# First mixer of a two-layer trunk: one softmax division moved into the head's norm, and rotations and value splits done on pairs of tiles

## The chip, the cores and the metric

The kernel runs on one core of one Trainium2 chip. The metric is the device time of one execution in microseconds (us). The core's engines each follow their own instruction list in order and wait for one another by semaphores: TensorE (PE in the profile, with its weight loads as PEld), VectorE (DVE), ScalarE (ACT), GpSimd (POOL) and SyncE (SP), which here issues most of the DMAs.

## The reference, cut to what matters

The reference is a trunk of two layers on a sequence of 256 rows of width 1024, with a context of 256 rows. Only the first layer's mixer is touched: differential attention with 8 heads (128 value columns each, two maps of 64 columns), joined with a gated unit and followed by a product with `w_out`. All of it is float32.

```python
q_x, k_x, v_x, gu_x, gv_x = split(hx @ w_in)          # rows of x
k_c, v_c = split(hc @ w_in[:, ...])                    # rows of the context
q_x, k_x = apply_rope(q_x), apply_rope(k_x)            # rotate halves of 64 columns
k_all, v_all = concat([k_c, k_x]), concat([v_c, v_x])  # 512 rows
# per block of 128 query rows and head, m = 0, 1:
p = softmax(q[m] @ k[m].T * scale)                     # 128 x 512, two maps
a = p[0] - lam * p[1]
o = a @ v                                              # 128 x 128
# head_rms:
o = o * rsqrt(mean(o * o) + 1e-5) * g * (1 - lam_init)
```

After the mixer come a norm, a PEER block (top-k routing over 16384 experts), and the second layer with a pooling mixer and another PEER block. None of that changes.

## The kernel before, in words

All weight matrices stream in as "items": tiles of 128x1024 float32. For each item SyncE loads a `raw` tile (four buffers, line 54), ScalarE copies it to a rounded `hi` (line 61) and VectorE subtracts to get `lo` (line 63); there are three `hi`/`lo` pairs (`RING`). A product is then three matmul passes, hi by hi, hi by lo and lo by hi. `run_items` writes the order by hand: for each item it first emits the splits of up to two items ahead (`ahead`), then the item's matmuls (`run`), then work that was put off by the item before (`settle` runs what `defer` collected), then the item's `after`. The engines' lists follow this order of emission, so what stands behind a waiting instruction on its engine waits too.

The first mixer works in four groups g of two heads. A group is six items:

- two k items (t = 0, 1). `transposed` (line 598) makes 24 matmuls of 256 columns for the rows of x into `p[:, :256]` and 24 for the context into `p[:, 256:]`; p is one of three PSUM buffers of one bank (`pa`). In `after`, `rope` rotates the x half, and `parts` splits the context half with one ScalarE copy (line 154) and one VectorE subtraction (line 155).
- two q items: 24 matmuls each into half a bank, then `rope`.
- two v items, of which the second does all the work: four blocks b of 24 matmuls (line 837), each into a bank of its own and each with its own `parts`.

`rope` (lines 678 to 691) swaps groups of 32 partitions with four ScalarE copies from PSUM into `sw` (line 683), multiplies p by a table row on VectorE (line 685), and defers four more VectorE steps, `rest`: a multiplication (688), an addition (689), and the split into hi and lo (193, 194). Its two scratch tiles have three buffers each. Both engines read the same bank here, and the framework puts accesses of two engines to one bank one behind the other.

The attention itself is cut into 20 "units" (`unit`, called by `units`), one at a time beside the items: in group g at four places (k item 0, k item 1, blocks 0 and 2 of v), and for units 13 to 19 in the first items of the product with `w_out`. Unit u makes the scores of (head, query block) number u, transposes those of u - 2 (`turn`), multiplies by v for a finished head (`mix`), and at u = 7, 11, 15, 19 takes the norm of a group (`rms`). `scores` (lines 694 to 715) does six matmuls into two banks and then, for each map m: VectorE's negated maximum (707), ScalarE's exponential with the row sum in a column (709), VectorE's reciprocal of that sum (710). Then VectorE scales the second reciprocal by -lam (712), the second map by it (713), and adds the first map times its reciprocal (714).

Beside this VectorE adds up three vectors from `ada_w` (`ada_step`: one step loads a 128x1024 tile `aw` into one of three buffers, line 366, and does one multiply-add over the tile loaded before it, line 375; two steps after each k item, one after others). At the end of a vector TensorE takes column sums (line 382). After the last unit's norm the memory of the attention is closed, and only then SyncE loads the residual rows and `grow` (line 876) for the norm that follows the mixer (line 219).

Of the kernel before, what the change touches and what calls it, by code (L numbers as in the profile page):

```python
# [11 lines left out]
FT = mybir.dt.float32  # L12
# [22 lines left out]
class Build:  # L35
# [425 lines left out]
    def first(self):  # L461
# [216 lines left out]
        def rope(dst, h, p, x):  # L678
            T = st["K"]

            sw = T.tile([128, 256], FT, name="rp", bufs=3)
            for r in range(0, 128, 32):
                nc.scalar.activation(sw[r:r + 32], p[r ^ 32:(r ^ 32) + 32], AF.Copy)
            t = T.tile([128, 256], FT, name="rt1", bufs=3)
            nc.vector.tensor_mul(t, p, st["rope"][:, x, 0])

            def rest():
                nc.vector.tensor_mul(sw, sw, st["rope"][:, x, 1])
                nc.vector.tensor_add(t, t, sw)
                self.split_v(dst[0][:, h, :256], dst[1][:, h, :256], t)  # L690
            self.defer(rest)


        def scores(g, h, nb):
            T = st["T"]
            s = slice(128 * nb, 128 * nb + 128)
            mx = T.tile([128, 2, 4], FT, name="amx", bufs=3)
            e = []
# [7 lines left out]
            for m, p in enumerate(ps):  # L706
                nc.vector.tensor_reduce(mx[:, m, 0:1], p, axis=AX.X, op=OP.max, negate=True)
                x = T.tile([128, 512], FT, name="ex", bufs=6)
                nc.scalar.activation(x, p, AF.Exp, bias=mx[:, m, 0:1], accum_out=mx[:, m, 2:3])
                nc.vector.reciprocal(mx[:, m, 3:4], mx[:, m, 2:3])  # L710
                e.append(x)
            nc.vector.tensor_mul(mx[:, 1, 3:4], mx[:, 1, 3:4], st["nlam"])
            nc.vector.tensor_scalar(e[1], e[1], mx[:, 1, 3:4], None, op0=OP.mult)
            nc.vector.scalar_tensor_tensor(e[0], e[0], mx[:, 0, 3:4], e[1], op0=OP.mult, op1=OP.add)
# [28 lines left out]
        def rms(g):  # L743
# [3 lines left out]
            for h in range(2):  # L747
                for nb in range(2):
                    nc.tensor.matmul(p[:, 2 * h + nb:2 * h + nb + 1], sq[:, h, 128 * nb:128 * nb + 128], self.ones,
                                     start=True, stop=True)  # L750
            ms = T.tile([128, 4], FT, name="ms", bufs=2)
            nc.vector.tensor_scalar(ms, p[:, :4], 1.0 / 128, EPS, op0=OP.mult, op1=OP.add)
# [31 lines left out]
        for g in range(4):  # L784
            for t in range(2):
                def run(hi, lo, t=t, g=g):
                    p = self.pa()
                    transposed(hi, lo, [(p[:, :256], self.h)])
                    if g and t == 0:
                        self.settle()  # L790
                        units()
                    transposed(hi, lo, [(p[:, 256:], hc)])
                    st["p"] = p

                def after(g=g, t=t):
                    if t == 0:
                        T = st["K"]
                        st["k", g] = [T.tile([128, 2, 512], FR, name=f"kT{i}", bufs=2) for i in range(2)]
                        st["q", g] = [T.tile([128, 2, 256], FR, name=f"qT{i}", bufs=2) for i in range(2)]
                    ada_step(2)  # L800
                    k = st["k", g]
                    rope(k, t, st["p"][:, :256], 0)
                    self.parts(k[0][:, t, 256:], k[1][:, t, 256:], st["p"][:, 256:])
# [10 lines left out]
            for t in range(2):  # L814
                def run(hi, lo):
                    st["p"] = self.pa()
                    transposed(hi, lo, [(st["p"][:, :256], self.h)])

                def after(g=g, t=t):
                    ada_step()  # L820
                    rope(st["q", g], t, st["p"][:, :256], 1)
                self.item(w[n], run, after=after)
                n += 1
            for t in range(2):
                def run(hi, lo, t=t, g=g):
# [5 lines left out]
                    for b in range(4):  # L831
                        p = self.pa()[:, :256]
# [6 lines left out]
                        self.parts(v[0][:, b], v[1][:, b], p)  # L839
# [612 lines left out]
```

## Time and profile before

| | |
|---|---|
| time, median of 3 runs | 2065.9 us (2065.89 to 2066.82) |
| the profiled execution | 2066.66 us, span 2064.7 us |
| mean granted TensorE clock | 0.978 of full speed |
| PE busy | 1977.2 us (96%) |
| DVE busy | 1572.4 us (76%) |
| ACT busy | 978.5 us (47%) |
| POOL busy | 379.1 us (18%) |
| DMA | 389.93 MB, 189 GB/s over the span |

The span runs from the first to the last instruction of the profiled execution. A busy share is an average over stages with different limits. Times inside a stage are given from the start of the span; the groups of the first mixer lie between some 65 and 252 us, its product with `w_out` from there to some 308 us. Ends of matmuls are modelled, so that neighbouring matmuls overlap on paper. In a timeline row the first two numbers are start and duration, and a bracket tells how long the engine had been idle before it and what released it. In a row of waits the three numbers are the total, the count and the longest.

### The profile page before, as it was taken

The numbers are of one execution on the slowest core, as the hardware profiler recorded it, in microseconds if no ns is written. First come the engines' busy times: TensorE is split into PE (matmuls) and PEld (weight loads), VectorE is DVE, ScalarE is ACT, GpSimd is POOL, SyncE is SP. The second block draws the span as 40 slices with busy tenths as digits, with TensorE's granted clock in tenths as the row PEclk, the third lists the DMA queues.
The fourth block names the chain that finished last, engine by engine and source line by source line (L and its number), as shares of the span: only waits on it lengthen the run. The fifth ranks groups of instructions, "written<-read, shape, count | busy, mean of one in ns | idle before, by whom it ended". The sixth has DMA issues, their size and how long they took to land.

```text
span 2064.7 us, 34190 instructions
## 1 busy us (share of the span) xinstructions
PE 1977.2 (96%) x13348; PEld 1781.8 (86%) x13348; DVE 1572.4 (76%) x2820; ACT 978.5 (47%) x1398; POOL 379.1 (18%) x171
## 2 busy tenths in 40 slices
PE   8899888999999999999999889999999999999997
PEld 4888767999999998888878679999999998888886
DVE  6878867999888857777776767999888755555566
ACT  6444435454544444444445454454544444444443
POOL 0100006785000000000011427892000000000031
PEclk9999998999999999999999989999999999999999
DMA  8533244455444457888876445555444555665663
GB/s 305 209 134 133 82 143 164 154 176 172 156 156 149 154 190 258 289 293 305 285 275 214 175 142 174 168 180 164 154 154 147 172 183 193 193 195 193 212 232 128
DMA packets 108177, 389.93 MB, mean 189 GB/s; under 512 B 12776, under 2 KB 12904, under 8 KB 108016
## 3 DMA queue, kind: packets, MB, share of 16 engines
q1 hardware_dynamic: 105992, 384.37, 55.3%
q10 hardware_dynamic: 2024, 3.38, 0.5%
q8 instruction: 104, 1.70, 0.3%
q14 instruction: 57, 0.47, 0.1%
HBM read 384.55 MB, written 3.16 MB: 188 GB/s over the span
## 4 chain that ended last, share of the span: by engine, by line
PE 63%; DVE 26%; issue 6%; ACT 3%; DMA 1%; POOL 1%; SPq 0%; ACTq 0%; DVEq 0%; POOLq 0%
PE pa L311 25%; PE px L311 8%; PE pa L941 8%; PE pa L945 7%; PE pa L942 7%; DVE lo L63 2%; PE pt L1093 2%; ACT hi L61 1%; DVE oh L1020 1%; DVE oh L1025 1%; DVE topi L971 1%; DVE sc L972 1%; DVE topi L974 1%; PE pa L837 1%; DVE idx L1026 1%
## 5 line engine op out<-in xcount | busy, mean ns | idle before, releaser
L61 ACT ACTIVATE hi<-raw 128x1024 fp32r<-128x1024 f32 x599 | 633.0, 1059 | 573.7 <-PE px L311 359.6
L63 DVE TENSOR_TENSOR lo<-raw,hi 128x1024 fp32r<-128x1024 f32 x487 | 614.1, 1263 | 363.6 <-ACT hi L61 362.3
L941 PE MATMUL pa<-h,hi 128*128 128x256 f32 x2304 | 578.1, 289 | 2.1 <-DVE h L280 2.1
L942 PE MATMUL pa<-h,hi 128*128 128x256 f32 x2304 | 566.4, 284 | 0.5 <-DVE h L281 0.5
L311 PE MATMUL pa<-hi,h 128*128 128x512 f32 x1524 | 472.1, 391 | 1.3 <-ACT h L278 1.2
L941 PEld LDWEIGHTS pa<-h,hi 128*128 128x128 f32 x2304 | 442.0, 192 | 2.9 <-DVE h L280 2.9
L942 PEld LDWEIGHTS pa<-h,hi 128*128 128x128 f32 x2304 | 442.9, 192 | 1.0 <-issue 1.0
L311 PEld LDWEIGHTS pa<-hi,h 128*128 128x128 f32 x1524 | 286.3, 188 | 64.1 <-issue 1.7
L945 PE MATMUL pa<-h,lo 128*128 128x256 f32 x2304 | 323.6, 283 | 0.0
L63 POOL TENSOR_TENSOR lo<-raw,hi 128x1024 fp32r<-128x1024 f32 x112 | 287.8, 2587 | 79.2 <-ACT hi L61 78.8
L945 PEld LDWEIGHTS pa<-h,lo 128*128 128x128 f32 x2304 | 298.1, 192 | 0.0
L311 PE MATMUL pa<-lo,h 128*128 128x512 f32 x762 | 255.7, 390 | 0.0
L1227 POOL TENSOR_SCALAR ln_g<-ln_g 128x1024 f32<-128x1024 f32 x2 | 5.6, 2776 | 1144.0 <-DMA ln_g<-in_ln_g 1144.0
L311 PE MATMUL px<-hi,h 128*128 128x512 f32 x508 | 197.7, 389 | 0.0
L311 PEld LDWEIGHTS pa<-lo,h 128*128 128x128 f32 x762 | 143.4, 188 | 30.0
L1107 ACT ACTIVATE A<-pt 128x256 f32<-128x256 f32 (+31 forms) x182 | 50.9, 310 | 226.6 <-DVE A L1105 217.4
L311 PEld LDWEIGHTS px<-hi,h 128*128 128x128 f32 x508 | 95.3, 188 | 19.7
L1084 DVE TENSOR_TENSOR m<-e,gd 128x512 f16<-128x512 f16 x256 | 105.2, 452 | 2.2
L311 PE MATMUL px<-lo,h 128*128 128x512 f32 x254 | 98.8, 389 | 0.0
L375 DVE SCALAR_TENSOR_TENSOR aacc<-aw,csil,aacc 128x1024 f32<-128x1024 f32 x70 | 89.4, 1278 | 0.1
L1093 PE MATMUL pt<-m,e 128*128 128x128 f16 x1024 | 81.6, 220 | 3.1 <-DVE m L1084 0.7
L155 DVE TENSOR_TENSOR h<-A,h 128x1024 fp32r<-128x1024 f32 (+1 forms) x66 | 81.0, 1227 | 1.4 <-ACT h L154 1.4
(369 smaller groups left out, 2178.5 us busy)
## 6 DMA issues: line engine op xcount, KB each, us to landing
raw<-in_uT SPq DMA_DIRECT2D x256, 512.0 KB, 3.5
raw<-in_peer_v SPq DMA_DIRECT2D x256, 512.0 KB, 4.3
aw<-in_ada_w SPq DMA_DIRECT2D x80, 512.0 KB, 5.4
raw<-in_w_in SPq DMA_DIRECT2D x32, 512.0 KB, 4.7
raw<-in_wq SPq DMA_DIRECT2D x32, 512.0 KB, 3.7
raw<-in_ab_w_out SPq DMA_DIRECT2D x12, 512.0 KB, 3.5
raw<-in_ada_w SPq DMA_DIRECT2D x8, 512.0 KB, 5.7
xraw<-in_ada_w SPq DMA_DIRECT2D x8, 512.0 KB, 4.9
```

What stands on the lines that cost most here:

```text
L61: nc.scalar.activation(hi, it["raw"], AF.Copy)
L63: eng.tensor_sub(lo, it["raw"], hi.bitcast(FT))
L155: self.nc.vector.tensor_sub(lo, src, hi.bitcast(FT))
L311: nc.tensor.matmul(acc[2 * nb + a // 512], s[x], w[:, a:b], start=i == 0 and part == 0, stop=i == last and part == 2)
L375: nc.vector.scalar_tensor_tensor(st["acc"], w, c, st["acc"], op0=OP.mult, op1=OP.add)
L837: nc.tensor.matmul(p, h(k, s)[x], tiles[k // 4][y][:, 256 * (k % 4):256 * (k % 4) + 256], start=part == 0 and k == 0, stop=part == 2 and k ...
L941: mm(out, hi[:, cs], hh, start=k == 0, stop=False)
L942: mm(out, hi[:, cs], hl, start=False, stop=False)
L945: mm(out, lo[:, cs], self.h(k)[0], start=False, stop=k == 7)
L1084: nc.vector.tensor_tensor(v4(x), v4(st["e1"][:, s]), wide(st["gd"][i], ch, 4), op=OP.mult)
L1093: nc.tensor.matmul(p[:, 128 * j:128 * j + 128], e2[:, j], m[i][:, j], start=i == 0, stop=i == 1)
L1107: nc.scalar.activation(x[:, e:], y[:, e:], AF.Copy, scale=1.0 / 4096)
```

## The change

- `scores`: the first map is no longer divided by its sum. Its sums go to a tile of four columns per group (`asum`). The second map is scaled by (first sum / second sum) times -lam and added to the undivided first map, so a head's output is too large by the first sum. One reciprocal and one pass over 128x512 fall away; the other small step takes two column operands.
- `rms`: the head's norm divides that factor out. For this the small constant in the norm is multiplied by the squared sum: two VectorE steps on 128x4 where there was one.
- k items: the x halves of both items go into one bank and the context halves into another; `rope` and `parts` then run once for the pair, in the second item's `after`, on 512 columns. q items: both into one bank, `rope` once for the pair. The scratch tiles of `rope` have one buffer of twice the size.
- v blocks: two blocks share a bank, and `parts` runs once for two.

The matmuls, the splits of weight tiles and all DMAs stay as they are.

```diff
-        def rope(dst, h, p, x):
+        def rope(dst, p, x):
+
             T = st["K"]
-            sw = T.tile([128, 256], FT, name="rp", bufs=3)
+            sw = T.tile([128, 2, 256], FT, name="rp", bufs=1)
             for r in range(0, 128, 32):
                 nc.scalar.activation(sw[r:r + 32], p[r ^ 32:(r ^ 32) + 32], AF.Copy)
-            t = T.tile([128, 256], FT, name="rt1", bufs=3)
-            nc.vector.tensor_mul(t, p, st["rope"][:, x, 0])
+            t = T.tile([128, 2, 256], FT, name="rt1", bufs=1)
+
+            def row(i):
+                return st["rope"][:, x, i][:, None].to_broadcast([128, 2, 256])
+            nc.vector.tensor_mul(t, p, row(0))
             def rest():
-                nc.vector.tensor_mul(sw, sw, st["rope"][:, x, 1])
+                nc.vector.tensor_mul(sw, sw, row(1))
                 nc.vector.tensor_add(t, t, sw)
-                self.split_v(dst[0][:, h, :256], dst[1][:, h, :256], t)
+                self.split_v(dst[0][:, :, :256], dst[1][:, :, :256], t)
...
+            if h == nb == 0:
+                st["sum", g] = T.tile([128, 4], FT, name="asum", bufs=3)
+            sums = st["sum", g][:, 2 * h + nb:2 * h + nb + 1], mx[:, 1, 2:3]
...
-                nc.scalar.activation(x, p, AF.Exp, bias=mx[:, m, 0:1], accum_out=mx[:, m, 2:3])
-                nc.vector.reciprocal(mx[:, m, 3:4], mx[:, m, 2:3])
+                nc.scalar.activation(x, p, AF.Exp, bias=mx[:, m, 0:1], accum_out=sums[m])
                 e.append(x)
-            nc.vector.tensor_mul(mx[:, 1, 3:4], mx[:, 1, 3:4], st["nlam"])
-            nc.vector.tensor_scalar(e[1], e[1], mx[:, 1, 3:4], None, op0=OP.mult)
-            nc.vector.scalar_tensor_tensor(e[0], e[0], mx[:, 0, 3:4], e[1], op0=OP.mult, op1=OP.add)
+            nc.vector.reciprocal(mx[:, 1, 3:4], sums[1])
+            nc.vector.tensor_scalar(mx[:, 1, 3:4], mx[:, 1, 3:4], st["nlam"], sums[0], op0=OP.mult, op1=OP.mult)
+            nc.vector.scalar_tensor_tensor(e[0], e[1], mx[:, 1, 3:4], e[0], op0=OP.mult, op1=OP.add)
...
+            sm = st.pop(("sum", g))
             ms = T.tile([128, 4], FT, name="ms", bufs=2)
-            nc.vector.tensor_scalar(ms, p[:, :4], 1.0 / 128, EPS, op0=OP.mult, op1=OP.add)
+            nc.vector.scalar_tensor_tensor(sm, sm, EPS, sm, op0=OP.mult, op1=OP.mult)
+            nc.vector.scalar_tensor_tensor(ms, p[:, :4], 1.0 / 128, sm, op0=OP.mult, op1=OP.add)
...
                 def run(hi, lo, t=t, g=g):
-                    p = self.pa()
-                    transposed(hi, lo, [(p[:, :256], self.h)])
+                    if t == 0:
+                        st["pk"] = [self.pa() for _ in range(2)]
+                    cs = slice(256 * t, 256 * t + 256)
+                    transposed(hi, lo, [(st["pk"][0][:, cs], self.h)])
...
-                    transposed(hi, lo, [(p[:, 256:], hc)])
-                    st["p"] = p
+                    transposed(hi, lo, [(st["pk"][1][:, cs], hc)])
                 def after(g=g, t=t):
-                    if t == 0:
+                    ada_step(2)
+                    if t:
...
-                    ada_step(2)
-                    k = st["k", g]
-                    rope(k, t, st["p"][:, :256], 0)
-                    self.parts(k[0][:, t, 256:], k[1][:, t, 256:], st["p"][:, 256:])
+                        p = [x.rearrange("p (a b) -> p a b", a=2) for x in st["pk"]]
+                        rope(k, p[0], 0)
+                        self.parts(k[0][:, :, 256:], k[1][:, :, 256:], p[1])
...
                     ada_step()
-                    rope(st["q", g], t, st["p"][:, :256], 1)
+                    if t:
+                        rope(st["q", g], st["p"].rearrange("p (a b) -> p a b", a=2), 1)
...
-                        p = self.pa()[:, :256]
+                        if b % 2 == 0:
+                            pv = self.pa()
+                        p = pv[:, 256 * (b % 2):256 * (b % 2) + 256]
...
-                        self.parts(v[0][:, b], v[1][:, b], p)
+                        if b % 2:
+                            self.parts(v[0][:, b - 1:b + 1], v[1][:, b - 1:b + 1], pv.rearrange("p (a b) -> p a b", a=2))
```

## Rows read from the trace of the kernel before

**Rows 1.** The page's chain of work that ended last, as shares of the whole span by engine.

```profile
PE 63%; DVE 26%; issue 6%; ACT 3%; DMA 1%; POOL 1%; SPq 0%; ACTq 0%; DVEq 0%; POOLq 0%
```

**Rows 2.** Busy time by stretch: the stretch, its length, then busy us and instructions of each engine, the granted clock, the DMA share and GB/s. The four stretches are those of the mixer from the v block of group 0 into the product with `w_out`.

```profile
93.00:131.00 38.00, 34.22 (x246) 30.37 (x246) 29.85 (x55) 14.17 (x31) 0.00 (x0) 0.96 0.47 159
131.00:177.00 46.00, 41.34 (x286) 38.17 (x287) 37.38 (x70) 21.79 (x50) 0.00 (x0) 0.85 0.44 149
177.00:230.00 53.00, 46.98 (x368) 43.47 (x366) 42.90 (x87) 23.90 (x53) 0.00 (x0) 0.97 0.32 110
230.00:278.00 48.00, 42.23 (x256) 35.50 (x257) 37.47 (x93) 22.86 (x49) 0.00 (x0) 0.89 0.24 77
```

**Rows 3.** Who waited for whom between 78 and 310 us: total us, times, longest.

```profile
DVE amx L710 <- ACT ex L709: 27.5, 32, 1.2
ACT kT L154 <- DVE rt L685: 17.6, 7, 4.2
...
PE pa L837 <- ACT hi L61: 11.9, 6, 3.7
...
PE pa L837 <- DVE lo L63: 4.7, 3, 3.2
...
DVE nlam L510 <- ACT sl L508: 1.1, 1, 1.1
...
DVE amx L707 <- PE pt L705: 0.4, 1, 0.4
```

**Rows 4.** VectorE's timeline over one unit of scores, from the first maximum to the first instruction behind the unit.

```profile
244.02 0.68 DVE L707 TENSOR_REDUCE amx<-pt 128x1 f32<-128x512 f32 x1
245.55 0.16 DVE L710 RECIPROCAL amx<-amx 128x1 f32<-128x1 f32 x1 [0.84 <-ACT ex L709]
245.63 0.67 DVE L707 TENSOR_REDUCE amx<-pt 128x1 f32<-128x512 f32 x1
247.15 0.16 DVE L710 RECIPROCAL amx<-amx 128x1 f32<-128x1 f32 x1 [0.85 <-ACT ex L709]
...
248.06 0.75 DVE L714 SCALAR_TENSOR_TENSOR ex<-ex,amx 128x512 f32<-128x512 f32 x1
248.73 0.75 DVE L155 TENSOR_TENSOR v<-pa,v 128x256 fp32r<-128x256 f32 x2
```

**Rows 5.** ScalarE's timeline in the same unit.

```profile
246.34 0.69 ACT L709 ACTIVATE ex<-pt,amx 128x512 f32<-128x512 f32 x1 [0.82 <-DVE amx L707]
246.92 0.19 ACT L709 ACTIVATION_READ_ACCUMULATOR ex<-pt,amx 128x1 f32 x1
247.01 0.65 ACT L154 ACTIVATE v<-pa 128x256 fp32r<-128x256 f32 x2
```

**Rows 6.** Groups of instructions between 100 and 330 us by line and shape: busy us, mean ns of one | idle before.

```profile
L683 ACT ACTIVATE rp<-pa 32x256 f32<-32x256 f32 x48 | 18.0, 376 | 5.3 <-PE pt L705 4.6
L154 ACT ACTIVATE aT<-pt 128x512 fp32r<-128x512 f32 x16 | 9.6, 597 | 2.6 <-PE pt L724 2.5
...
L194 DVE TENSOR_TENSOR cat<-og,cat 128x512 fp32r<-128x512 f32 x4 | 2.8, 692 | 0.1
L759 DVE TENSOR_TENSOR og<-og,pt 128x512 f32<-128x512 f32 x4 | 2.7, 678 | 0.0
...
L194 DVE TENSOR_TENSOR kT<-rt,kT 128x256 fp32r<-128x256 f32 x6 | 2.6, 425 | 0.2
...
L193 DVE CAST kT<-rt 128x256 fp32r<-128x256 f32 x6 | 1.8, 294 | 0.2
...
L193 DVE CAST cat<-og 128x512 fp32r<-128x512 f32 x4 | 1.7, 426 | 0.1
...
L185 DVE TENSOR_SCALAR rs_t<-rs_t,rs_r 128x1 f32<-128x1 f32 x2 | 0.4, 212 | 0.1
```

**Rows 7.** VectorE's timeline around the first k item of group 3.

```profile
219.50 0.41 DVE L685 TENSOR_TENSOR rt<-pa,rope 128x256 f32<-128x256 f32 x1
220.36 0.42 DVE L155 TENSOR_TENSOR kT<-pa,kT 128x256 fp32r<-128x256 f32 x1 [0.45 <-ACT kT L154]
221.31 1.22 DVE L63 TENSOR_TENSOR lo<-raw,hi 128x1024 fp32r<-128x1024 f32 x1 [0.52 <-ACT hi L61]
222.45 0.42 DVE L688 TENSOR_TENSOR rp<-rp,rope 128x256 f32<-128x256 f32 x1
...
224.03 1.28 DVE L375 SCALAR_TENSOR_TENSOR aacc<-aw,csil,aacc 128x1024 f32<-128x1024 f32 x1
```

**Rows 8.** TensorE's timeline: where a product with v began late, and the end of a k item in group 2.

```profile
93.82 1.22 PE L837 MATMUL pa<-lo,h 128*128 128x256 f32 x4 [3.18 <-DVE lo L63]
...
163.36 1.12 PE L598 MATMUL pa<-hc,lo 128*128 128x256 f32 x8
...
231.34 1.22 PE L837 MATMUL pa<-hi,h 128*128 128x256 f32 x4 [3.72 <-ACT hi L61]
```

**Rows 9.** VectorE's timeline in groups 0 and 2: two steps of `ada` after the second k item of group 0, and the first multiplication of `rope` for the first k item of group 2.

```profile
78.12 2.60 DVE L375 SCALAR_TENSOR_TENSOR aacc<-aw,csil,aacc 128x1024 f32<-128x1024 f32 x2
...
167.36 0.42 DVE L685 TENSOR_TENSOR rt<-pa,rope 128x256 f32<-128x256 f32 x1
```

**Rows 10.** DMA issues by line between 60 and 290 us: count, KB each, median us from issue to landing.

```profile
aw<-in_ada_w SPq DMA_DIRECT2D x24, 512.0 KB, 5.1
```

**Rows 11.** SyncE's timeline: two loads for `ada` in group 0, with the time that their issue took.

```profile
73.40 1.79 SPq L366 DMA_DIRECT2D aw<-in_ada_w  x2
```

More of the change, by code (lines that the diff above doesn't have):

```diff
@@ L791, in run @@
                         units()
-                    transposed(hi, lo, [(p[:, 256:], hc)])
-                    st["p"] = p
+                    transposed(hi, lo, [(st["pk"][1][:, cs], hc)])
                 def after(g=g, t=t):
-                    if t == 0:
+                    ada_step(2)
+                    if t:
                         T = st["K"]
-                        st["k", g] = [T.tile([128, 2, 512], FR, name=f"kT{i}", bufs=2) for i in range(2)]
+                        k = st["k", g] = [T.tile([128, 2, 512], FR, name=f"kT{i}", bufs=2) for i in range(2)]
                         st["q", g] = [T.tile([128, 2, 256], FR, name=f"qT{i}", bufs=2) for i in range(2)]
-                    ada_step(2)
-                    k = st["k", g]
-                    rope(k, t, st["p"][:, :256], 0)
-                    self.parts(k[0][:, t, 256:], k[1][:, t, 256:], st["p"][:, 256:])
+                        p = [x.rearrange("p (a b) -> p a b", a=2) for x in st["pk"]]
+                        rope(k, p[0], 0)
+                        self.parts(k[0][:, :, 256:], k[1][:, :, 256:], p[1])
                     if g and t:
@@ L814, in first, with run @@
             for t in range(2):
-                def run(hi, lo):
-                    st["p"] = self.pa()
-                    transposed(hi, lo, [(st["p"][:, :256], self.h)])
+                def run(hi, lo, t=t):
+                    if t == 0:
+                        st["p"] = self.pa()
+                    transposed(hi, lo, [(st["p"][:, 256 * t:256 * t + 256], self.h)])
                 def after(g=g, t=t):
                     ada_step()
-                    rope(st["q", g], t, st["p"][:, :256], 1)
+                    if t:
+                        rope(st["q", g], st["p"].rearrange("p (a b) -> p a b", a=2), 1)
                 self.item(w[n], run, after=after)
```

## The prediction

> **What bounds the kernel now.** I read the chain of waits first. Over the whole span it lies 63% on TensorE and 26% on VectorE [rows 1], and the page's 96% for PE would say that work on VectorE is free. That is an average over stages, so next comes the table of stretches for the mixer alone. There TensorE is idle for 38 - 34.2 = 3.8, 4.7, 6.0 and 5.8 us of the four stretches, 20.3 us together, and its granted clock is below one in all four [rows 2]. The two levels are 2.4 and 1.2 GHz. A mean clock of 0.85 over 46 us is 6.9 us of full-speed time lost, and 1.5, 1.6 and 5.3 in the others: 15.3, some of it inside the idle time. TensorE could therefore be 20 to 35 us faster here if it were never kept waiting.
>
> Then the list of waits, to see who keeps it waiting. Its products with v waited 11.9 us for `hi` and 4.7 for `lo` [rows 3], and the gaps stand at the first v block of a group (3.2 and 3.7 us) [rows 8]. The reverse wait hardly exists: VectorE waited 0.4 us for score matmuls [rows 3]. What VectorE does wait for is ScalarE: 27.5 us in 32 waits before the reciprocals, 0.85 us each. In group 2 TensorE had finished both k items at 164.5 us [rows 8], while VectorE came to the rotation of the first one at 167.4 [rows 9]. So from about 102 to 283 us VectorE's list, with its waits for the exponentials in it, is the limit, and TensorE stands still when `lo` or a tile behind it comes late. Time taken out of that list should move the end until TensorE itself is the limit.
>
> **The change, part by part, on VectorE's list.**
>
> *Scores.* A unit takes 248.73 - 244.02 = 4.71 us [rows 4]. Now both maxima are issued one behind the other and nothing between them waits. The exponential starts 0.71 after its maximum (245.63 to 246.34), the next ScalarE instruction can start 0.67 later (246.34 to 247.01), and the reciprocal follows its exponential by 0.81 (246.34 to 247.15) [rows 4, 5]. So the one reciprocal comes at 0.71 + 0.67 + 0.81 = 2.19. Then 0.20 for it, 0.25 for the small step with two column operands (0.21 long [rows 6]), and 0.67 for the last pass up to the next instruction (248.06 to 248.73). That is 3.31, a gain of 1.40 per unit, 22.4 in 16. The bounds: if the second maximum still had to wait for the first exponential, because both write one small tile, the unit would take 0.71 + 0.81 + 0.71 + 0.81 + 1.12 = 4.16 and the gain be 8.8. With a small step of 0.16 it is 23. I take 22.4; no instruction shown here lets me see the first of these cases.
>
> *Rotations.* On 256 columns one takes about 1.92: 1.58 for the deferred part (222.45 to 224.03 [rows 7]) and 0.34 for the first multiplication. By durations two of them are 2 x (0.41 + 3 x 0.425 + 0.294) = 3.96; on 512 columns it is 0.678 + 3 x 0.692 + 0.426 = 3.18 [rows 6]. I take 0.7 per pair, since neighbours overlap by some 0.1, and 5.6 for eight pairs. That no row shows a table row read twice by one instruction bounds it between 0 (two runs at the old price) and 6.4. On ScalarE the four copies go from 4 x 0.376 to 4 x about 0.6 per pair (the 512-column copy is 0.597 [rows 6]), 2.4 for 3.0; ScalarE is not the limit, so I count nothing.
>
> *Context halves of k.* Today ScalarE's copy of the context half waits for VectorE's multiplication of the x half, 17.6 us in seven waits [rows 3], because the two halves share a bank. VectorE then waits 0.45 for that copy, and again 0.52 for the `hi` that stands behind the copy on ScalarE [rows 7]. In the changed kernel the halves lie in two banks, and the copy can run early. I count 8 x 0.45 = 3.6, 4 x 0.5 = 2.0, and 4 x 0.15 for one subtraction in place of two. The table load for the exponential in group 0 stands behind the same copy, so VectorE's 1.1 us wait for `nlam` [rows 3] goes too.
>
> *Split of v and the norm.* Two subtractions of about 0.68 replace four of 0.42 per group, less overlap 0.15: 0.6 in all. The norm's extra step on four columns costs 0.2 four times: +0.8. Bounds for both together are minus 1 and plus 1.
>
> Sum on VectorE: 22.4 + 5.6 + 3.6 + 2.0 + 0.6 + 1.1 + 0.6 - 0.8 = 35.1 us.
>
> *What moves.* The rotation of the first k item now waits for the second item's matmuls. That costs nothing while VectorE comes to it later anyway, as in group 2 above. The Trainium skill speaks against it: PSUM — Partial Sum Buffer, in its section "PSUM bank collisions raise a hardware error", asks that two engines not touch one bank at a time, so a bank that holds both tiles can't be emptied while TensorE fills its second half. By that rule alone each pair would put about one k item of TensorE work in front of VectorE, some 6 us four times; the rows in which VectorE is behind say about zero, and the sum takes zero.
>
> A real cost is the order: all deferred steps of the k pair (2.5 us for 1.58) now stand between the two `lo` tiles that the first v block needs. That is 0.95 later per group, 3.8 in all.
>
> *From VectorE's sum to the end.* In the four stretches lie 15 units (21.0), seven pairs (4.9), six of the 0.45 and three of the 0.5 waits (4.2), and 0.5 net of the small terms: 30.6. Against it stand the 3.8, about 2 where VectorE will now reach the column sums of `ada` before TensorE has made them, and about 3 for hand-overs where the two engines are level, my estimate from the single gaps of 0.5 to 1 us. That leaves 21.8, inside TensorE's room of 20 to 35. In group 0 the gain is small: the second `ada` step after the k pair needs a tile issued at about 73.4 [rows 11] that takes 5.1 us [rows 10], so it can't start before 78.5, and it starts at 79.4 today [rows 9]. I count 0.9, plus 1.2 for the waits behind it, less the 0.95 already charged: 1.2. Unit 15, behind the stretches, gives 1.4. Together 21.8 + 1.2 + 1.4 = 24.4. What follows the mixer is the same program and only starts earlier. The profiled execution took 2066.7, 0.8 above the median of 2065.9: 2066.7 - 24.4 = 2042.3, and I say 2042.
>
> **The rivals.**
>
> 1. TensorE or the `hi` tiles become the limit early, and half of the gain is lost. For it: the stretches have only 20.3 us of plain idle time, and the clock may stay low. Against: a low clock came with gaps. Price: the waits for `hi` and `lo` alone are 16.6; with 4 us of them left the gain is about 12.6: 2054.
> 2. The second maximum still waits for the first exponential. The gain falls by 22.4 - 8.8 = 13.6 to 10.8: 2056. Against: the two use different columns.
> 3. No change: VectorE's time is hidden after all, as the page's 96% for PE has it. Against: the waits of PE in the mixer. 2063 to 2069.
> 4. Slower. The swap's scratch tile now has one buffer. The copies of the q pair on ScalarE can't start before the addition for the k pair has read it, and VectorE's multiplication waits for all four copies. Between that addition and the multiplication stand a cast, a subtraction, two `ada` steps and a `lo`, about 0.46 + 0.61 + 2 x 1.2 + 1.13 = 4.6 us, against 2.4 of copies, so by these rows nothing waits, and in group 3, with no `ada` steps left, 2.2 against 2.4. It decides only if `rope` waits 35.1 / 8 = 4.4 us or more per pair. At most it is the copies at 4 x 0.75 = 3.0 and the deferred 2.5, 5.5 for each of eight pairs: 44 - 35 = 9 slower, 2076.
>
> That the pairs are not run as such (two runs of 256 inside an instruction) is the lower bound of the rotation's term: 5.6 less, 2048, within the forecast's own range.
>
> **How the numbers follow.** The forecast, 18 to 32 us faster (2035 to 2049), has 0.63; rival 1 0.22; rival 2 0.05; rival 3 0.05; rival 4 0.05. About 4 us, 0.2%, is what a measurement of this kernel can tell from no change. Faster by more than that: 0.63 + 0.22 + 0.05 = 0.90; within: 0.05; slower: 0.05. The range 2034 to 2057 takes in the forecast and rivals 1 and 2, and leaves out rivals 3 and 4 and the tails.
>
> **What would show it.** In the changed kernel's profile: 16 reciprocals in the mixer, each behind a wait of about 0.9 us, and no second pass over 128x512; 32 copies of 32x512 at about 0.6; no wait of ScalarE's context copy for `rope`'s multiplication; PE idle time in the mixer's stretches clearly under 20 us with a higher granted clock; the product with `w_out` beginning some 22 us earlier, and later stages with unchanged lengths. Wrong would be: maxima that still stand 1.6 us apart, a wait of VectorE's first rotation step for the copies in most pairs, or TensorE gaps at the first v block as long as today.

## The result, and the profile after

The changed kernel takes 2044.1 us (median of 4 runs, 2043.39 to 2045.52) against 2065.99 us of the kernel before in the same comparison: a ratio of 0.989, with the interval 0.9878 to 0.9902, or 22 to 23 us (20 to 25 by the interval). The forecast was 2042 in 2034 to 2057. Its profiled execution has a span of 2042.5 us, 22.2 less than before.

The page after: the busy time of the engines, and the chain of work that ended last.

```profile
PE 1963.7 (96%) x13348; PEld 1773.0 (87%) x13348; DVE 1559.4 (76%) x2740; ACT 970.3 (48%) x1354; POOL 377.9 (19%) x171
...
PE 64%; DVE 25%; issue 5%; DMA 2%; ACT 2%; POOL 1%; SPq 0%; DVEq 0%; ACTq 0%; POOLq 0%
```

Both lines look as they did [rows 1]: 96% for PE and 76% for DVE before and after, while the time fell by 1.1%. Nothing can be learnt here from shares of the whole span; the stage has to be read. (`x2740` is 80 instructions fewer on VectorE.)

VectorE's timeline over one unit of scores after the change (line numbers have moved: maxima 715, reciprocal 719, the small step 720, the last pass 721).

```profile
187.56 1.28 DVE L715 TENSOR_REDUCE amx<-pt 128x1 f32<-128x512 f32 x2
189.76 0.16 DVE L719 RECIPROCAL amx<-amx 128x1 f32<-128x1 f32 x1 [0.92 <-ACT ex L717]
189.96 0.27 DVE L720 TENSOR_SCALAR amx<-amx,nlam,asum 128x1 f32<-128x1 f32 x1
190.27 0.75 DVE L721 SCALAR_TENSOR_TENSOR ex<-ex,amx 128x512 f32<-128x512 f32 x1
190.94 0.68 DVE L155 TENSOR_TENSOR v<-pa,v 128x512 fp32r<-128x512 f32 x1
```

It is the counterpart of [rows 4]: the two maxima stand in one row (`x2`), one wait of 0.92 is left of two, and the unit takes 190.94 - 187.56 = 3.38 us in place of 4.71.

The waits of the changed kernel between 78 and 289 us, as in [rows 3].

```profile
ACT rp L684 <- DVE rt L693: 16.7, 4, 10.7
DVE amx L719 <- ACT ex L717: 14.9, 16, 1.0
PE pa L852 <- DVE lo L63: 13.6, 5, 4.7
...
DVE aacc L375 <- DMA aw<-in_ada_w: 4.1, 1, 4.1
...
DVE aw L390 <- PE pt L389: 3.2, 2, 3.0
DVE amx L715 <- PE pt L713: 3.0, 2, 2.4
...
DVE adac L383 <- PE pt L382: 2.3, 1, 2.3
...
PE pa L852 <- ACT hi L61: 1.5, 2, 1.3
DVE rt L689 <- ACT rp L684: 1.0, 1, 1.0
```

Three things are to be seen. The waits for the exponentials fell from 27.5 us in 32 to 14.9 in 16. ScalarE's wait of 17.6 us with the context copy is gone. And there are new ones: VectorE now waits 13.6 us (4.1 + 3.2 + 3.0 + 2.3 + 1.0) for the load of an `ada` tile, for TensorE's sums of `ada` (lines 382, 389) and scores, and for ScalarE's copies of `rope`. The list of before has 1.1 us for the same causes (0.4, 0.2 and 0.5). TensorE's own waits at the v blocks hardly shrank, 11.9 for `hi` and 4.7 for `lo` before, 1.5 and 13.6 now; what changed is where they lie. These are three of them, in groups 0, 1 and 3:

```profile
88.46 1.22 PE L852 MATMUL pa<-lo,h 128*128 128x256 f32 x4 [4.67 <-DVE lo L63]
...
135.51 0.74 PE L852 MATMUL pa<-lo,h 128*128 128x256 f32 x4 [3.21 <-DVE lo L63]
...
220.34 0.74 PE L852 MATMUL pa<-lo,h 128*128 128x256 f32 x4 [0.88 <-DVE lo L63]
```

All brackets of this kind added up, the gaps at the v blocks of groups 0 to 3 were 6.8, 3.4, 1.3 and 5.1 us before and are 8.3, 4.7, 1.3 and 0.9 now.

Where the new waits stand, in VectorE's timeline: groups 0, 1 and 2.

```profile
79.50 1.28 DVE L375 SCALAR_TENSOR_TENSOR aacc<-aw,csil,aacc 128x1024 f32<-128x1024 f32 x1 [4.13 <-DMA aw<-in_ada_w]
...
119.66 0.68 DVE L390 TENSOR_TENSOR aw<-pt,aw 1x512 f32<-1x512 f32 x1 [3.04 <-PE pt L389]
...
165.59 0.17 DVE L383 TENSOR_TENSOR adac<-pt,adabc 128x8 f32<-128x8 f32 x1 [2.29 <-PE pt L382]
```

When each group's work reached TensorE: the start of the first k item of group 3 and of the product with `w_out`, before

```profile
201.18 2.03 PE L598 MATMUL pa<-h,hi 128*128 128x256 f32 x15
...
252.09 1.19 PE L311 MATMUL pa<-hi,cat 128*128 128x512 f32 x4
```

and after.

```profile
193.33 1.91 PE L598 MATMUL pa<-h,hi 128*128 128x256 f32 x14
...
235.18 1.19 PE L311 MATMUL pa<-hi,cat 128*128 128x512 f32 x4
```

Group 0 gains nothing (its successor starts at 105.92 after 105.56), group 1 about 1 (151.29 to 150.69 at its end), groups 2 and 3 bring 7.2 and 9.1, and the units inside the product with `w_out` the rest. In the two groups that gained little the gaps at the v blocks grew. VectorE comes to the norm behind the mixer (line 219) 302.75 - 281.47 = 21.3 us earlier, which is nearly the whole 22.2 of the span.

Busy time by stretch, after, as in [rows 2]; the fourth stretch ends at 258 us in place of 278, since the work in it now ends some 20 us earlier.

```profile
93.00:131.00 38.00, 36.23 (x257) 32.48 (x258) 27.96 (x40) 14.03 (x26) 0.00 (x0) 0.93 0.45 153
131.00:177.00 46.00, 42.45 (x331) 39.32 (x330) 38.43 (x57) 24.36 (x46) 0.00 (x0) 0.96 0.50 171
177.00:230.00 53.00, 51.10 (x411) 48.07 (x412) 46.73 (x89) 23.75 (x46) 0.00 (x0) 1.00 0.35 121
230.00:258.00 28.00, 26.79 (x164) 21.37 (x163) 22.76 (x50) 15.87 (x35) 0.00 (x0) 1.00 0.24 75
```

TensorE is idle for 1.8 + 3.5 + 1.9 + 1.2 = 8.4 us of these 165. In the first three stretches alone it was 14.5 before and is 7.2 now. The granted clock is at full speed in the last two, and in the second 0.96 after 0.85; in the first it fell from 0.96 to 0.93, although the idle time there halved.

### The profile page after: what moved, and what is told of

It reads as the page before. It is cut to its first block, busy times and chain, and to the rows that moved or that the text cites. A ratio compares the mean times of both kernels' runs of the same rounds, so it can differ in the third digit from the quotient of the medians.

```text
span 2042.5 us, 34071 instructions
## 1 busy us (share of the span) xinstructions
PE 1963.7 (96%) x13348; PEld 1773.0 (87%) x13348; DVE 1559.4 (76%) x2740; ACT 970.3 (48%) x1354; POOL 377.9 (19%) x171
## 3 DMA queue, kind: packets, MB, share of 16 engines
q10 hardware_dynamic: 2024, 3.38, 0.6%
## 4 chain that ended last, share of the span: by engine, by line
PE 64%; DVE 25%; issue 5%; DMA 2%; ACT 2%; POOL 1%; SPq 0%; DVEq 0%; ACTq 0%; POOLq 0%
PE pa L311 26%; PE px L311 8%; PE pa L957 8%; PE pa L958 8%; PE pa L961 8%; PE pt L1109 2%; DVE lo L63 2%; DVE oh L1036 1%; DVE oh L1041 1%; DVE topi L987 1%; DVE sc L988 1%; PE pa L598 1%; DVE topi L990 1%; PE pa L852 1%; ACT hi L61 1%
```

## The experiments

All were run in five rounds, each ratio against the kernel before on the same chip. Microseconds won are (1 - ratio) x 2066. The intervals reach some 2 to 3 us to either side, so two experiments can be told apart from about 0.002 (4 us) on. Where an experiment's own profile is used, that is said.

### The two halves of the change

**Scores and norm alone** (`e1`): the kernel before with the new `scores` and `rms`.

```diff
-                nc.scalar.activation(x, p, AF.Exp, bias=mx[:, m, 0:1], accum_out=mx[:, m, 2:3])
-                nc.vector.reciprocal(mx[:, m, 3:4], mx[:, m, 2:3])
+                nc.scalar.activation(x, p, AF.Exp, bias=mx[:, m, 0:1], accum_out=sums[m])
...
+            nc.vector.reciprocal(mx[:, 1, 3:4], sums[1])
```

> The kernel before with the change of scores and of the norm alone; rotations and splits stay on single tiles. If VectorE's list with its waits for the exponentials sets the end, each of 16 units of scores is 4.71 - 3.38 = 1.33 us shorter, 21.3 us in all, less 0.8 for the norm; in the changed kernel 35 us on VectorE gave 22 us at the end, so about 0.65 of it should arrive: 13 us faster, 2053 (2050 to 2056). If only the removed instructions count and not the wait (one pass of 0.49 us and two small steps of 0.16 per unit), it is 0.8 x 16 x 0.65 = 8, 2058. If the parts work only together, less than 4 us.

Measured: 2047.75 us, ratio 0.9909 (0.9893 to 0.9924), 18.8 us won. More than expected: of the 21.3 us that 16 units save by the unit's length, 88% arrive at the end.

**Pairs alone** (`e2`): the changed kernel with the old `scores` and `rms`.

```diff
-            nc.vector.reciprocal(mx[:, 1, 3:4], sums[1])
...
+                nc.vector.reciprocal(mx[:, m, 3:4], mx[:, m, 2:3])
```

> The changed kernel with the scores and the norm of before. If VectorE's list sets the end: 14 us shorter on VectorE (rotations 5.6, waits around the context copy 5.6, the wait for nlam 1.1, the rest small), times 0.65, about 8 us faster, 2058 (2054 to 2061). The rival: the pair's deferred steps stand between the two lo tiles of the first v block, 0.95 later in each of four groups, and the pairs bring nothing or cost: 2064 or more.

Measured: 2061.81 us, 0.9974 (0.9964 to 0.9985), 5.4 us won. Faster, though less than the 8 expected. Since 18.8 + 5.4 = 24.2 against 22.7 for both, the halves don't disturb each other by more than the intervals allow. The waits of `e2` are needed further down:

```profile
PE pa L847 <- DVE lo L63: 13.9, 5, 3.6
...
DVE amx L711 <- PE pt L709: 4.5, 4, 2.2
...
PE pa L847 <- ACT hi L61: 2.4, 2, 2.2
...
PE pt L382 <- DVE aacc L375: 0.7, 1, 0.7
```

### Which part of the scores

**Both maxima first** (`e3`): the kernel before, with the maxima issued ahead of both exponentials; every reciprocal and pass stays.

```diff
             for m, p in enumerate(ps):
                 nc.vector.tensor_reduce(mx[:, m, 0:1], p, axis=AX.X, op=OP.max, negate=True)
+            for m, p in enumerate(ps):
                 x = T.tile([128, 512], FT, name="ex", bufs=6)
```

> The kernel before with one thing changed: both maxima are issued before the two exponentials and reciprocals; all instructions stay. If the wait for the exponentials is the larger part of the scores' gain, a unit goes from 4.71 to about 3.8 us, 14 us on VectorE, 0.65 of it at the end: 9 us faster, 2057 (2054 to 2060). If the removed pass over 128x512 is what counts, it is within 3 us of the kernel before.

Measured: 2051.91 us, 0.9929 (0.9915 to 0.9942), 14.7 us won from one moved line. The gain expected, 9 us, was too small: a miss. The wait itself, in this experiment's waits:

```profile
ACT kT L154 <- DVE rt L685: 17.5, 7, 4.2
DVE amx L711 <- ACT ex L710: 12.5, 32, 0.6
```

27.5 - 12.5 = 15.0 us of waiting fell away, and 14.7 were won. The other big wait of the list (17.5 on ScalarE) is untouched.

**The wait put back** (`e7`): the changed kernel with a reciprocal of the first sum between the maxima. Nothing reads its result.

```diff
                 nc.scalar.activation(x, p, AF.Exp, bias=mx[:, m, 0:1], accum_out=sums[m])
+                nc.vector.reciprocal(mx[:, m, 3:4], sums[m])
                 e.append(x)
-            nc.vector.reciprocal(mx[:, 1, 3:4], sums[1])
```

> The changed kernel with the reciprocal of the first sum put back between the two maxima, its result unused: the pass over 128x512 stays away, only the wait is back. If the wait is what the new scores mainly save, a unit goes from 3.38 to about 4.3 us and the end is 12 us later, 2056 (2053 to 2059). If the removed pass is what counts, it is at most 4 us later.

Measured: 2057.05 us, 0.9952 (0.9938 to 0.9965): 12.8 us lost against the changed kernel, by 16 instructions of 0.16 us. Its waits show why:

```profile
DVE amx L718 <- ACT ex L717: 27.5, 32, 0.9
```

That is the 27.5 of before again, 12.6 more than the changed kernel has. From both sides, then, some 13 to 15 of the 18.8 us are the wait, and the rest is the pass and the small steps.

### Which part of the pairs

**The context copy first** (`e5`): the kernel before, with ScalarE's copy of the context half issued ahead of `rope`'s copies and multiplication.

```diff
+                    nc.scalar.activation(k[0][:, t, 256:], st["p"][:, 256:], AF.Copy)
                     rope(k, t, st["p"][:, :256], 0)
-                    self.parts(k[0][:, t, 256:], k[1][:, t, 256:], st["p"][:, 256:])
+                    nc.vector.tensor_sub(k[1][:, t, 256:], st["p"][:, 256:], k[0][:, t, 256:].bitcast(FT))
```

> The kernel before with one order changed: ScalarE copies the context half of k before the four copies of the rotation, so the copy no longer waits for VectorE's multiplication in the same bank; nothing is paired. If the price given to the shared bank is right (0.45 us in 8 k items and 0.5 behind it in 4, on VectorE, whose time has been arriving nearly in full), it is 5 us faster than the kernel before (3 to 6). The rival: these waits of 0.45 were covered by others, and it is within 2 us.

Measured: 2062.48 us, 0.9974 (0.9963 to 0.9985), 5.4 us won, as expected. In its waits no row of ScalarE behind `rope`'s multiplication is left, nor VectorE's 3.1 us for that copy. So the order in the shared bank cost the kernel before 5.4 us (3 to 8 by the interval), and moving one line wins as much as all pairs.

**Two scratch buffers** (`e6`): the changed kernel with two of each of `rope`'s scratch tiles, the place of rival 4.

```diff
-            sw = T.tile([128, 2, 256], FT, name="rp", bufs=1)
+            sw = T.tile([128, 2, 256], FT, name="rp", bufs=2)
...
-            t = T.tile([128, 2, 256], FT, name="rt1", bufs=1)
+            t = T.tile([128, 2, 256], FT, name="rt1", bufs=2)
```

> The changed kernel with two scratch buffers for the rotations instead of one, and no other change. If the single buffer costs nothing, because VectorE always has 4 us of other work between the two uses, it is within 1.5 us of the changed kernel's 2044. The rival (the buffer ties ScalarE's q copies and the hi behind them to VectorE): 3 us faster or more, and then the buffer, not the order, made the gain of e4.

Measured: 2043.2 us, 0.9888 (0.9872 to 0.9903) against 0.989. The 16.7 us that ScalarE waits for the one buffer in the changed kernel cost nothing that can be measured: ScalarE has the time.

**The rest one item later** (`e4`): the changed kernel, with the four deferred steps of the k pair put behind the second `lo` tile; as two pairs are then open, with the two buffers of `e6`.

```diff
-            self.defer(rest)
+            self.defer(rest if x else lambda: self.defer(rest))
```

> The changed kernel, with the deferred steps of the k pair put off by one more item, so that both lo tiles of the first v block come before them on VectorE; two scratch buffers instead of one, so that the q pair's copies need not wait. If the order on VectorE matters, most of the 13.6 us that v products waited for lo goes in groups 0 and 1 and the end comes 5 us earlier: 2039 (2036 to 2042). If only VectorE's sum counts, it is within 2 us of the changed kernel's 2044.

Measured: 2038.27 us, 0.9859 (0.9844 to 0.9874), as expected; 0.0029 below `e6`, that is 6 us (2 to 10) from the order alone. So I took it as shown that the 0.95 per group that the prediction charges for `lo` is a real cost, only larger. The next run doesn't bear that out for the pairs alone.

**Pairs alone, the rest later** (`e9`): the same move in `e2`.

> The kernel of e2 (pairs alone, scores of before) with the k pair's deferred steps one item later and two scratch buffers. If e2 gave only 5 us because these steps stand between the two lo tiles of the first v block, the pairs now bring 10 to 12 us against the kernel before: 2056 (2054 to 2058). The rival: VectorE simply saves less by pairs than counted, and it stays within 2 us of e2, ratio 0.997.

Measured: 2060.44 us, 0.997 (0.9958 to 0.9982) against 0.9974 of `e2`. A miss. TensorE's waits for `lo` did fall, from 13.9 to 6.7 us, and the time stayed. These are `e9`'s waits:

```profile
PE pa L847 <- DVE lo L63: 6.7, 3, 4.5
...
PE pa L847 <- ACT hi L61: 4.3, 4, 2.2
DVE aacc L375 <- DMA aw<-in_ada_w: 4.0, 1, 4.0
PE pt L382 <- DVE aacc L375: 3.9, 1, 3.9
...
DVE adac L383 <- PE pt L382: 2.3, 1, 2.3
DVE amx L711 <- PE pt L709: 1.9, 1, 1.9
...
DVE rt L689 <- ACT rp L684: 1.0, 1, 1.0
DVE aw L390 <- PE pt L389: 0.9, 2, 0.7
```

TensorE's waiting did not fall, it moved: it waits more for `hi` (4.3 after 2.4) and for the multiply-add ahead of the column sums (3.9 after 0.7). From 76 us to 4.5 before line 219, the busy time (the first number with a count) leaves TensorE idle for 24.4 us in `e2` and for 25.5 in `e9`:

```profile
76.00:292.07 216.07, 191.69 (x1309) 170.58 (x1307) 170.61 (x310) 92.59 (x167) 0.00 (x0) 0.91 0.37 127
...
76.00:291.89 215.89, 190.43 (x1308) 170.17 (x1307) 170.47 (x311) 91.62 (x167) 0.00 (x0) 0.93 0.38 127
```

VectorE waits 10.1 us in the five rows of its own, and 9.9 in `e2` (4.5 for scores, 2.6, 1.0, 0.9, 0.9). This gave a new theory: look at VectorE's own waits. In the kernel before the first k item's rotation and split stood ahead of the second item's `ada` steps and gave the load, the copies and the sums time to arrive. With that work moved into the second item's `after`, VectorE comes to the `ada` steps too early.

**The ada steps behind the pair** (`e11`): `e9`, with the second k item's two `ada` steps issued after `rope` and `parts`.

```diff
                 def after(g=g, t=t):
-                    ada_step(2)
-                    if t:
+                    if not t:
+                        ada_step(2)
+                    else:
...
                         self.parts(k[0][:, :, 256:], k[1][:, :, 256:], p[1])
+                        ada_step(2)
```

> The pairs with the old arithmetic of the scores (the run of pairs with their rest one item later, 2060.4), and in the second key item the two ada steps issued behind the rotations and the splits instead of ahead of them. If the pairs alone bring little because VectorE, with the first item's rotations gone, comes to its ada steps before the transfer, the copies and the column sums that they read (waits of 4.0, 0.9 + 1.0 and 2.3 + 1.9 us in that run's groups 0 to 2), work put ahead of the steps takes 3 to 5 us off: about 2056, ratio 0.995. If the time is lost elsewhere, within 1.5 us of 2060.4, and the waits stand at the steps as before.

Measured: 2055.89 us, 0.9946 (0.9932 to 0.9959), 0.0024 below `e9`: 5 us, at the upper end of what was expected. Its waits:

```profile
DVE amx L711 <- PE pt L709: 2.8, 1, 2.8
...
DVE aacc L375 <- DMA aw<-in_ada_w: 1.9, 1, 1.9
...
DVE adac L383 <- PE pt L382: 1.3, 1, 1.3
```

The rows for the copies and for the row sums are gone, the load's fell from 4.0 to 1.9. So work ahead of the steps, as cover for what they read, is worth some 3 to 5 us to the pairs. The move also brings the rotations and splits forward by two steps; what that alone is worth wasn't tested.

### Towards a faster version

**Ada tiles loaded two ahead** (`e8`): `e4` with the load issued two steps before its use. The loads keep their places in the list, and each multiply-add comes one step later.

```diff
-... ("col", self.adac[:, 0, j])))
+... ("col", self.adac[:, 0, j])), ahead=2)
```

> The kernel of e4 (deferred steps of the k pair one item later) with the tiles of ada loaded two steps ahead instead of one. If the 3 us that VectorE waited for a tile of ada in group 0 sets the begin of the first v block, the end comes 2 us earlier than e4, 2036 (2034 to 2038). The rival: TensorE waits there for something else, and it is within 1 us of e4.

Measured: 2035.53 us, 0.9845 (0.9832 to 0.9859). The wait for the load goes from 3.1 us to 1.0, and 3 us are won, as expected; the intervals of the two overlap, so the times alone don't settle it.

**The gate later** (`e10`): `e8`, with VectorE's work on the mixer's spatial gate (and the exponentials of lambda) in group 0 moved from the second k item to the second q item.

```diff
-                    elif t:
-                        lam_exp()
-                        for nb in range(2):
-                            spatial(nb)
...
                         rope(st["q", g], st["p"].rearrange("p (a b) -> p a b", a=2), 1)
+                    if t and not g:
+                        lam_exp()
+                        for nb in range(2):
+                            spatial(nb)
```

> The kernel of e8 with the gated unit's VectorE work of group 0 (about 5 us) moved from behind the second k item to behind the second q item, so that it comes after both lo tiles. If VectorE's sum is what is left as the limit, it is within 1.5 us of e8's ratio (0.9845). If order in group 0 still matters, it is 3 us faster.

Measured: 2039.01 us, 0.9872 (0.9857 to 0.9887): slower than `e8` by 3.5 us (medians) to 5.6 (ratios), a miss. VectorE's waits other than for the exponentials are 9.3 us here and 6.3 in `e8`. The added ones are 0.5 for the load, 0.8 for the sums' row 390 and 1.7 for v. That suggests that the gate's passes had been cover as well.

**Both** (`e12`): `e8` with the `ada` steps behind the pair, as in `e11`.

> The same move of the ada steps on the fastest kernel so far (the changed kernel with the rest one item later, two scratch buffers and the ada tiles loaded two ahead, 2035.5). Few of VectorE's waits at the steps are left there (copies 3.0 us, transfer 1.0, row sums 1.1): if they go, 1 to 4 us faster, 2033; if the end there is set by TensorE and the weight tiles' halves, within 1.5 us of 2035.5.

Measured: 2032.5 us, 0.9828 (0.9814 to 0.9841): 35 us faster than the kernel before and 12 to 13 us faster than the changed one. The earlier load and the place of the `ada` steps might serve the kernel before as well; that wasn't tried. Against `e8` it is 3.5 us, again with intervals that overlap. VectorE's rows for the load, the sums of `ada` and `rope`'s copies are all gone from its waits. The window from 76 us to 4.5 before line 219 shows what is left, here for `e12`:

```profile
76.00:264.09 188.09, 178.12 (x1317) 159.74 (x1317) 162.81 (x283) 91.22 (x169) 0.00 (x0) 1.00 0.44 148
```

TensorE is busy in 178.1 of 188.1 us at full clock: at most some 10 us can still be had here by feeding it better.

### One account for all

An engine's time is made up of its busy time, its waits and the gaps between instructions. So the start of line 219, which is VectorE's, must move by the change of the three, whatever limits the stage: the table below can't show that VectorE is the limit (`e3` and `e7` do that), but it tells where each kernel's time went. Busy time is read in the window just shown: here it is for the kernel before

```profile
76.00:298.25 222.25, 193.17 (x1315) 171.13 (x1313) 178.09 (x363) 101.16 (x212) 0.00 (x0) 0.92 0.37 125
```

and after.

```profile
76.00:276.97 200.97, 182.34 (x1311) 162.97 (x1311) 163.46 (x283) 90.62 (x167) 0.00 (x0) 0.97 0.41 138
```

VectorE is the third number with a count. All columns are in us, from each kernel's own profile. "Exp" is the wait for exponentials, "others" every other wait of VectorE in the window except `lo` or `xlo` behind ScalarE; "sum" is the change of the three against the kernel before.

| kernel | busy | exp | others | sum | line 219 at | moved | won by ratio |
|---|---|---|---|---|---|---|---|
| before | 178.1 | 27.5 | 6.7 | | 302.8 | | |
| e5 copy first | 174.9 | 27.5 | 5.3 | -4.6 | 297.0 | -5.7 | 5.4 |
| e2 pairs alone | 170.6 | 27.2 | 10.5 | -4.0 | 296.6 | -6.2 | 5.4 |
| e9 pairs, rest later | 170.5 | 27.2 | 10.7 | -3.9 | 296.4 | -6.4 | 6.2 |
| e11 pairs, ada last | 170.3 | 27.2 | 7.4 | -7.4 | 293.3 | -9.4 | 11.2 |
| e7 wait back | 165.2 | 27.5 | 11.1 | -8.5 | 292.1 | -10.7 | 9.9 |
| e3 maxima first | 178.7 | 12.5 | 6.5 | -14.6 | 288.1 | -14.6 | 14.7 |
| e1 scores alone | 171.6 | 14.8 | 7.0 | -18.9 | 284.4 | -18.4 | 18.8 |
| after | 163.5 | 14.9 | 14.7 | -19.2 | 281.5 | -21.3 | 22.7 |
| e6 two buffers | 163.0 | 14.9 | 12.9 | -21.5 | 278.3 | -24.4 | 23.1 |
| e10 gate later | 162.4 | 14.8 | 9.3 | -25.8 | 274.8 | -27.9 | 26.4 |
| e4 rest later | 162.3 | 14.8 | 8.4 | -26.8 | 273.7 | -29.0 | 29.1 |
| e8 ada ahead | 161.4 | 14.9 | 6.3 | -29.7 | 270.9 | -31.8 | 32.0 |
| e12 both | 162.8 | 14.9 | 2.4 | -32.2 | 268.6 | -34.2 | 35.5 |

With pairs the sum falls short by 2 to 3 us each time. Of this, 0.9 to 1.5 is in the rows left out: the waits for `lo` and `xlo` behind ScalarE are 4.7 us before and 3.2 to 3.8 with pairs. The rest may be gaps between instructions, which are fewer there; that was not tested. A figure of the table is good to a few us only. `e5` removes no instruction of VectorE, and yet its busy time falls by 3.2, because five instructions more than before now lie ahead of 76 us:

```profile
76.00:292.51 216.51, 189.04 (x1305) 168.41 (x1304) 174.88 (x358) 99.42 (x208) 0.00 (x0) 0.94 0.38 126
```

Counted from the start of the span it is 230.0 us against 231.3. The pairs' miss is plain all the same: `e2` wins 7.5 us of busy time (6.6 from the start of the span) and pays 3.8 back in waits.

## Why the prediction was right

**What bounds the stage: right.** The forecast rested on VectorE's list being the limit from group 1 to the end of the mixer, against the page's 96% for PE. `e3` moves an order on VectorE alone, with every matmul and pass left in, and wins 14.7 us; `e7` takes 12.8 back. Rival 3 (no change) falls with them. It is less right for group 1, which gained only about 1 us, as group 0 gained nothing.

**Two of its signs failed.** The product with `w_out` begins 252.09 - 235.18 = 16.9 us earlier, not 22; the last 4 us are won inside it. And "TensorE gaps at the first v block as long as today", named as a sign of being wrong, came true in groups 0 and 1 (8.3 and 4.7 us after 6.8 and 3.4). The gain came from groups 2 and 3 and the product behind them.

**Scores, 22.4 forecast.** By the unit's length it is 4.71 - 3.38 = 1.33, 21.3 in 16; alone it brought 18.8 at the end. Of the steps of the sum the reciprocal came at 2.20 (forecast 2.19), and the small step with two column operands took 0.27 and 0.31 up to the next instruction, where 0.25 was taken from a row with one column. Rival 2 is refuted by the `x2` of the maxima: the second doesn't wait for the exponential that writes the same small tile.

**Rotations, 5.6 forecast.** By line and shape, after the change, between 78 and 310 us:

```profile
L684 ACT ACTIVATE rp<-pa 32x512 f32<-32x512 f32 x28 | 16.5, 589 | 26.5 <-DVE rt L693 16.7 <-DVE aw L390 7.8 <-PE pa L598 1.7
...
L693 DVE TENSOR_TENSOR rt<-rt,rp 128x512 f32<-128x512 f32 x8 | 5.5, 692 | 0.3
...
L689 DVE TENSOR_TENSOR rt<-pa,rope 128x512 f32<-128x512 f32 x8 | 5.5, 686 | 1.1 <-ACT rp L684 1.0
L692 DVE TENSOR_TENSOR rp<-rp,rope 128x512 f32<-128x512 f32 x8 | 5.5, 686 | 0.0
```

With the split's 428 and 693 ns the pair takes 0.686 x 2 + 0.692 + 0.428 + 0.693 = 3.19 where 3.18 was worked out, 0.77 less than two single ones (6.2 in eight), and a table row read twice by one instruction costs the same as any other 512 columns. The lower bound (nothing won) is off the table, and the copies on ScalarE are at the 0.6 assumed.

**Context halves, 3.6 + 2.0 forecast.** The first term holds: VectorE's wait for that copy, eight times 0.45 us, is gone, and `e5` prices the order in the shared bank at 5.4. The second was too large. It multiplied one wait of 0.52 for `hi` [rows 7] by four; there were three of them before (in groups 0, 1 and 3), and one of 0.39 is left: 1.2, not 2.0. A longer wait of that kind in the product with `w_out`, 2.3 us, stayed (2.5).

**One bank for a pair.** ScalarE's copies waited once for TensorE to fill a pair's bank (1.7 us in the row of line 684), and VectorE's multiplication once, 1.0, for those copies; the 6 us four times of the rule that spoke against the change don't appear. The Trainium skill (PSUM — Partial Sum Buffer, section "PSUM bank collisions raise a hardware error") asks that two engines keep off one bank at a time. The trace agrees in the other place: in the kernel before ScalarE's copy waited 17.6 us in seven for VectorE's multiplication in the same bank, and it was this order that cost time.

**Rival 4.** ScalarE does wait for the single buffer, 16.7 us, as that rival had it, but VectorE hardly waits for those copies (1.0 in all), and `e6` shows the price: none to be measured.

**VectorE's sum, 35.1 forecast.** By the account the move of 21.3 is 12.6 less waiting for exponentials, 5.6 less of old waits (3.1, 1.1 for `nlam`, the rest small), 13.6 of new waits, and 16.7 that is what remains: 14.6 of busy time and 2.1 that stands in none of the columns. Without the new waits it would be 34.9, or 33.8 if the 1.1 us that the kernel before had of them stay. The list was read right in the main. Part of the agreement is luck, since the scores and the waits for `hi` were put 1.1 and 0.8 too high.

**From that sum to the end: near in total, off inside.** The prediction took off 3.8 for the order of `lo`, 2 for column sums reached too early and 3 for hand-overs, and only 1.2 was left to group 0. Together with group 0 that is 35.1 - 24.4 = 10.7; the new waits are 13.6, and the kernel came out 2 us above the forecast. That the totals lie so close is in part luck. The sums of `ada` cost 3.2 + 2.3 = 5.5, not 2. The second `ada` step of group 0 starts at 79.50 where 78.5 was worked out, so 3.1 of its wait of 4.1 was foreseen. The waits for scores and copies, 3.0 + 1.0, stand where 3 was put down for hand-overs. And the 3.8 has no row on VectorE.

The step that missed the price is "The rotation of the first k item now waits for the second item's matmuls. That costs nothing while VectorE comes to it later anyway". It looked at the rotation, where the cost is 1.0 us in all, and not at the `ada` steps that lost the work ahead of them. `e11` gets 5 us back by restoring that cover. `e8` and `e12` get 3 and 3.5, with intervals that overlap, but with waits that fall by 2.1 and 3.9 in the traces.

What the order of `lo` costs stays open in part. In the changed kernel `e4` wins 6 us against `e6` by that move alone, which agrees with the 3.8. There VectorE's other waits fall from 12.9 to 8.4, by 2.5 for the scores and 1.4 for the column sums above all, and line 219 comes 4.6 us earlier; whether TensorE made these sooner because it no longer stood at `lo`, or VectorE came to them at a better moment, I didn't test. In the pairs alone (`e9`) the same move wins nothing that can be told from noise, and TensorE's waiting moved to other rows.

**Rival 1** was half there: TensorE still waited 15.1 us for `lo` and `hi`, where 16.6 was the figure before. It priced those waits as lost gain for the whole stage, and the gain did not halve. In groups 0 and 1, where the gaps stayed, next to nothing was won, so there it describes what happened.

**What follows the mixer.** From line 219 to the end of the span it is 1762.0 us before and 1761.0 after: unchanged, as said.

## What to carry to other kernels

When a page says that TensorE is 96% busy, look at a stage's waits and ask whose list the others wait for; a wait on that list can be worth as much as a busy microsecond. Then move that wait and see whether the end follows; adding up busy time and waits proves nothing by itself, since the two fill any engine's time. On an engine that works in order, issue both reductions before the first instruction that needs another engine's answer: here that alone was 14.7 of the 18.8 us. And when work is merged or moved, look at what used to stand behind it: the steps that now come earlier may reach a load or a sum that isn't there, and putting them behind the merged work, with one more step for the load to arrive, won some 6 of the 13 us that turned 22 into 35. The other 6 came from putting the deferred steps one item later (`e4`).

## What the runs showed that I had not expected

- One kind of wait can fall and come back as others: from `e2` to `e9` TensorE's wait for `lo` fell from 13.9 to 6.7 us, and its idle time in the stage went from 24.4 to 25.5. One 0.16 us reciprocal per unit (`e7`), in the wrong place, cost 12.8 us.
- The granted clock rose with edits that touched no matmul: a mean of 0.92 over the mixer before, 0.97 after and 1.00 in `e12`. With the two levels at 1.2 and 2.4 GHz, 0.92 over 222 us is by estimate 18 us of full speed lost. It doesn't simply follow the gaps: `e2` has less idle time than the kernel before (24.4 us after 29.1) and a clock of 0.91.
- A VectorE step on 128x1 with two column operands took 0.27 us, where a reciprocal of the same shape took 0.16.
